# A decoder layer with product-key experts on one NeuronCore: lists of expert rows in three classes instead of two, two dense rows less, and a new placing of gathers

## The chip, the cores and the metric

The kernel runs on one core of a Trainium2 chip. The metric is the device time of one execution in microseconds. Five engines work side by side, each in its own order: TensorE (PE in the profile, its weight loads PEld), VectorE (DVE), ScalarE (ACT), GpSimd (POOL) and SyncE (SP). SP, ACT and POOL also issue DMAs; gathers of rows by index are issued by POOL.

## The reference

One post-norm decoder layer on 256 tokens of 2048 features, all float32: attention of two kinds, an output projection with layer norm, then a product-key expert layer (PEER) with its layer norm, then a gated embedding with a third. The change touches the expert layer alone:

```python
va, ia = lax.top_k(sa, PEER_TOPK)          # 16 of 128 row keys, per token and head
vb, ib = lax.top_k(sb, PEER_TOPK)          # 16 of 128 column keys
top, sel = lax.top_k(cand, PEER_TOPK)      # 16 of the 256 sums
eidx = jnp.take_along_axis(cidx, sel, axis=-1)     # expert = ia * 128 + ib
gates = jax.nn.softmax(top, axis=-1)
act = jax.nn.gelu(jnp.einsum('thed,td->the', u[eb], xb))
out = jnp.einsum('the,thed->td', gates * act, v[eb])
```

There are 128 x 128 = 16,384 experts, each with one row of `u` and one of `v` (2048 float32, 8 KB). A token uses 8 heads x 16 experts.

## The kernel before, in words

The kernel treats the tokens in two ways. The first 88 tokens (`NSP`) are **sparse**: for each the 128 rows of `u` and of `v` are gathered by index, 128 rows at a time, and multiplied on VectorE (`sparse_work`, lines 1015 and 1025); that is 88 gathers of `u` rows and 88 of `v` rows (line 1049). A generator hands them out, and the numbers `GQ`, `GU`, `GUF`, `GUT`, `GUL`, `GUE` and `GV` say how many gathers are put into the order after each block of PE's work (`gathers(n)` adds n to an account and issues whole ones). Four buffers `gb` hold them, and the use of a gather is put into the order when the third one behind it is issued.

The other 168 tokens (`NDT`) are computed on TensorE, for all experts at once: 40 of them (`N0`) lie in the first tile of 128 tokens, 128 in the second. For every expert, W = gelu(u . x) times the token's gate (zero where the token did not choose it), and the output is the sum of W times `v`. In stages:

- **Dense u rows.** For the first `SEG1` of the 128 values of `ia`, all 128 experts are computed: one load of 1 MB, then 16 matmuls of 168 columns (`u_block`, line 223). Each float32 matmul is two instructions in the profile. The results stay in `A0` and `A1`.
- **Lists.** Beside that stage `list_work` counts which experts the 168 tokens really use, and packs their numbers densely into lists, 128 to a block (`idxV`). Part 1 covers the values of `ia` that were not computed densely, part 0 those that were. Experts used by second-tile tokens alone go into the first class, whose blocks need 128 columns; the experts that a first-tile token uses go into the second class, whose blocks take all 168 columns. `CAPS` fixes how many blocks each class has: `((24, 15), (30, 18))`. If a list overflows, a branch near the end (`tc.If(more > 0)`) computes what is left; with these inputs it is not taken.
- **u list.** For part 1, each block's `u` rows are gathered (`uf`, line 1412), transposed on TensorE (16 transposes, line 1453), copied out by ScalarE (`uT`, line 1456), and multiplied with the tokens (line 1462). ScalarE's gelu goes into `WL` (line 1494). Between these, `all_gates` works in small steps, `run(work, 1)`: `gate_work` turns the choices of three tokens at a time into one-hot matrices on VectorE (`eq`, `ohb`, line 717; `lo`, line 1105) and ScalarE (`hi`, line 1103), multiplies them on TensorE (lines 1114, 1115), and scales `A0`, `A1` or `WL` by the gates (line 1123). Then `A0` and `A1` are stored to DRAM as `s_w`.
- **v lists.** First part 0, then part 1: each block's `v` rows are gathered (`vf` or `vx`), for part 0 also the rows of `s_w` that belong to them (`wc`), and TensorE adds 16 products into six PSUM banks (`v_mm`, line 1512). A class says which columns a block writes (`cols`). Row buffers are five slots shared with the weights of other stages (`WF`) and four more, `vx` (`NVX`), that open once `A0` and `A1` are gone.
- At the end of part 1, `natural_out` (line 1071) and `third_sums` (line 1083) bring the sparse tokens' sums in, and layer norm and gate follow.

A scheduler places the instructions by a model of their times, but what goes through `keep` stays in the order written, engine by engine. VectorE's uses of the gathers, the one-hot matrices, ScalarE's `hi` and `uT` copies and all gathers on POOL are such. The order around the u list is written out in this loop (from line 1483):

```python
for b in range(NBLK[1]):
    for c in range(4):
        turn(4 * b + c + 2)                  # transposes, two chunks ahead
        rows_mm(ps, turned.pop(0), c, c0, n)
        if b >= 4 and (c or n > P) and not stored:
            run(work, 1)
    keep(nc.scalar.activation(WL_of(b), ps[:, :n], AF.Gelu_apprx_tanh))
    if b >= NBLK[1] - LEAD:
        fetch()                              # a v row block ahead
    gathers(GUL[n > P] if b < NBLK[1] - LEAD - 2 else GUE)
```

## Time and profile before

| | us |
|---|---|
| median of 3 runs | 1656.95 (1654.5 to 1661.91) |
| the profiled execution's own time | 1646.54 |
| its span, first to last instruction | 1644.7 |
| PE busy | 1604.3 (98%) |
| VectorE busy | 1058.7 (64%) |
| ScalarE busy | 731.3 (44%) |
| POOL busy | 583.1 (35%) |
| mean granted TensorE clock | 0.988 |

By the trace, dense u rows run from 532 to 813 us, the u list from 813 to 1139, the first v list from 1143 to 1319, the second from 1319 to 1536. The profile was taken of one execution; PE's busy time counts overlapping instructions once. A row of the order of time reads: start, length, engine, line, operation, output and inputs, shape, count of merged instructions, and in brackets the engine's idle time before it with what ended it. In shapes, "128*128 128x168" is a weight tile of 128 by 128 and 168 columns that stream through it. A row with a window has its start and end, its length, and the busy time and count of each engine named, then PEclk (the clock that TensorE was granted, 1.00 is full), the DMA engines' busy share and the GB/s they moved.

### The profile page before, as it was taken

To read this page: it belongs to the slowest core of one execution; us is meant where nothing else is said; L and a number is where in the kernel's file an instruction comes from. 1 tells how busy PE (TensorE), PEld (TensorE's weight loads), DVE (VectorE), ACT (ScalarE), POOL (GpSimd) and SP (SyncE) were. 2 spreads that over 40 slices of the span, in tenths; PEclk is the share of its full clock that TensorE was granted. 3 is DMA by queue.
4 is the path that set the end of the run, shared out by engine and by line. 5 is a ranking of instruction groups with operands and counts; after the bars stand their busy time and mean duration, and the time that the engine had idled before them with its cause. 6 is when DMAs were issued, how large, how long until landed. Compare 5 with 4: busy or idle time off the path is not lost. (4 is left out here: it accounts for less than half of the span.)

```text
span 1644.7 us, 30592 instructions
## 1 busy us (share of the span) xinstructions
PE 1604.3 (98%) x11666; PEld 1488.5 (91%) x11666; DVE 1058.7 (64%) x2557; ACT 731.3 (44%) x1740; POOL 583.1 (35%) x542
## 2 busy tenths in 40 slices
PE   9999999999999999999979999998899999999998
PEld 7888888888888999999979999998799999999786
DVE  5555588865378899577668778855476533341777
ACT  5587458753201264857646666632142000000543
POOL 0133123200233423322463434455878564440000
PEclk9999999999999999999989999999999999999999
DMA  8644654475799799999999999998999999996671
GB/s 295 203 157 162 230 172 142 154 287 187 282 409 412 285 421 403 410 375 385 371 387 376 343 349 355 360 401 356 408 406 384 366 402 420 421 402 210 214 260 51
DMA packets 90614, 518.53 MB, mean 315 GB/s; under 512 B 12308, under 2 KB 15444, under 8 KB 38322
## 3 DMA queue, kind: packets, MB, share of 16 engines
q0 software_dynamic: 47984, 330.83, 51.0%
q1 hardware_dynamic: 40750, 182.55, 30.4%
q10 hardware_dynamic: 1728, 3.15, 0.5%
q8 instruction: 92, 1.51, 0.4%
q14 instruction: 60, 0.49, 0.1%
HBM read 508.47 MB, written 10.18 MB: 315 GB/s over the span
## 5 line engine op out<-in xcount | busy, mean ns | idle before, releaser
L133 DVE TENSOR_TENSOR wl<-wf,wh 128x1024 fp32r<-128x1024 f32 (+1 forms) x199 | 212.8, 1092 | 126.9 <-ACT wh L132 125.5
L132 ACT CAST wh<-wf 128x1024 fp32r<-128x1024 f32 (+1 forms) x199 | 172.1, 892 | 243.3 <-DMA wf<-ple_gate 129.5
L1025 DVE SCALAR_TENSOR_TENSOR y<-gb,ew,y 128x2048 f32<-128x2048 f32 x78 | 183.2, 2349 | 127.7 <-DMA gb<-v_rows,eig 127.0
L223 PE MATMUL ps_u<-XF,wf 128*128 128x168 f32 x1632 | 251.1, 310 | 0.0
L223 PEld LDWEIGHTS ps_u<-XF,wf 128*128 128x128 f32 x1632 | 234.6, 190 | 2.2 <-DMA s_gl<-gl 0.2
L1462 PE MATMUL ps_u<-XF,uT 128*128 128x128 f32 (+1 forms) x1536 | 223.9, 290 | 0.2 <-ACT uT L1456 0.2
L1015 DVE SCALAR_TENSOR_TENSOR gb<-gb,xq 128x2048 f32<-128x2048 f32 x88 | 200.7, 2285 | 28.0 <-DMA gb<-u_rows,eig 27.9
L1462 PEld LDWEIGHTS ps_u<-XF,uT 128*128 128x128 f32 x1536 | 202.1, 193 | 0.7 <-ACT uT L1456 0.3
L1512 PE MATMUL ps_v<-WL,vf 128*128 128x128 f32 (+1 forms) x1536 | 196.1, 290 | 3.9 <-DMA vf<-v_rows,idxV 3.6
L1512 PEld LDWEIGHTS ps_v<-WL,vf 128*128 128x128 f32 x1536 | 193.7, 194 | 5.5 <-DMA vf<-v_rows,idxV 4.5
L1049 POOL DMA_INDIRECT gb<-u_rows,eig x88 | 99.6, 1132 | 242.6 <-DVE gb L1015 59.7
L211 PE MATMUL ps_qk<-X,wh 128*128 128x512 f32 x512 | 185.2, 401 | 0.0
L1456 ACT COPY uT<-ps_T 128x512 f32<-128x512 f32 x192 | 111.7, 586 | 106.3 <-PE ps_T L1453 106.1
L1103 ACT ACTIVATE hi<-eq,ghf 128x56 f16<-128x56 f16 (+2 forms) x336 | 87.3, 326 | 138.6 <-DVE eq L717 117.8
L213 PE MATMUL ps_qk<-X,wl 128*128 128x256 f32 x512 | 145.7, 285 | 0.0
L1412 POOL DMA_INDIRECT vf<-v_rows,idxV x73 | 93.9, 1286 | 120.6 <-PE ps_v L1512 88.2
L1049 POOL DMA_INDIRECT gb<-v_rows,eig x88 | 117.5, 1336 | 53.8 <-issue 20.7
L1453 PE MATMUL ps_T<-ident,uf 128*128 128x128 f32 x768 | 116.2, 276 | 5.8 <-ACT WL L1494 5.8
L211 PEld LDWEIGHTS ps_qk<-X,wh 128*128 128x128 f32 x512 | 96.4, 188 | 22.0 <-issue 1.0
L1512 PE MATMUL ps_v<-wc,vf 128*128 128x128 f32 (+1 forms) x800 | 107.3, 293 | 8.2 <-DMA vf<-v_rows,idxV 8.2
L223 PE MATMUL ps_q<-XF,wf 128*128 128x256 f32 x512 | 113.5, 379 | 0.0
L1512 PEld LDWEIGHTS ps_v<-wc,vf 128*128 128x128 f32 x800 | 102.6, 194 | 8.4 <-DMA vf<-v_rows,idxV 8.4
(366 smaller groups left out, 2859.3 us busy)
## 6 DMA issues: line engine op xcount, KB each, us to landing
wf<-peer_u SPq DMA_DIRECT2D x51, 1024.0 KB
wf<-w_qk SPq DMA_DIRECT2D x64, 512.0 KB
wf<-w_out SPq DMA_DIRECT2D x32, 512.0 KB
wf<-peer_wq SPq DMA_DIRECT2D x16, 1024.0 KB
wf<-ple_gate SPq DMA_DIRECT2D x16, 1024.0 KB
wf<-w_v SPq DMA_DIRECT2D x16, 512.0 KB
wf<-w_sv SPq DMA_DIRECT2D x15, 512.0 KB
early<-peer_u SPq DMA_DIRECT2D x5, 1024.0 KB
```

The costliest lines, as they stand in the source:

```text
L132: self.order(nc.scalar.copy(wh, src))
L133: self.order(nc.vector.tensor_tensor(wl, src, wh.bitcast(F32), op=ALU.subtract))
L211: nc.tensor.matmul(ps, wh[:, j * P:(j + 1) * P], xt[:, dt, :], start=dt == 0, stop=False)
L213: nc.tensor.matmul(ps[:, :T], wl[:, j * P:(j + 1) * P], xt[:, dt, :T], start=False, stop=dt == ND - 1)
L223: nc.tensor.matmul(ps[:, :T - t0], wf[:, dt * P:(dt + 1) * P], xt[:, dt, t0:], start=dt == 0, stop=dt == ND - 1)
L1015: keep(nc.vector.scalar_tensor_tensor(g, g, 1.0, xq[i], op0=ALU.mult, op1=ALU.mult, accum_out=eact[i][:, j:j + 1]))
L1025: keep(nc.vector.scalar_tensor_tensor(ys[i], g, ew[i][:, j:j + 1], ys[i], op0=ALU.mult, op1=ALU.add))
L1049: keep(nc.gpsimd.indirect_dma_start(out=g, out_offset=None, in_=a[kind], in_offset=bass.IndirectOffsetOnAxis(ap=eig[i][:, 0, j:j + 1], axi ...
L1453: nc.tensor.transpose(ps[:, j * P:(j + 1) * P], uf[:, (4 * c + j) * P:(4 * c + j + 1) * P], ident)
L1456: keep(nc.scalar.copy(uT, ps))
L1462: nc.tensor.matmul(ps[:, :n], uT[:, j * P:(j + 1) * P], XF[:, d, NSP + c0:NSP + c0 + n], start=d == 0, stop=d == ND - 1)
L1512: return nc.tensor.matmul(o, vf[:, d * P:(d + 1) * P], w, start=False, stop=last and (d % 3 == 2 or d == ND - 1))
```

## The change

- **Three classes.** A list now has experts used by second-tile tokens alone (blocks of 128 columns), by first-tile tokens alone (40 columns), and by both (168 columns), in this order (`SPAN`). Masks `m16`, `cols`, `used` and `inn` get a third layer; `CAPS` becomes `((23, 5, 10), (31, 7, 12))`, in blocks 38 and 50 for 39 and 48. `scale` gets the column at which a class begins, since classes 1 and 2 are adjacent for first-tile tokens, and classes 0 and 2 are not.
- **54 dense u rows** (`SEG1`) for 56.
- **Gathers.** Sparse gathers are left out in the first three u list blocks, and their paces change: `GUL` (1.28, 1.58) for (1.10, 1.50), `GUE` 1.75 for 2.20, `GV` (0.45, 0.82), (0.42, 0.98) for (0.42, 0.80), (0.42, 0.85). A 40-column block has the pace of a 128-column one.
- **High gate parts.** The three ScalarE multiplies that make `hi` are issued by `high` after the step's first `yield`, behind the next four transposes and eight matmuls, instead of together with `eq`.
- **First weight gathers.** `A0` and `A1` are closed and the first `wc` gathers issued after the last but one u list block, instead of after the last.
- **v slots.** The four `vx` buffers take the fifth to eighth v blocks instead of the sixth to ninth; four pairs of v and weight gathers instead of five go out ahead of the v loop.

The fallback branch is adapted to the new counts.

```diff
-SEG1 = 56
+SEG1 = 54
-CAPS = ((24, 15), (30, 18))
+CAPS = ((23, 5, 10), (31, 7, 12))
+NCL = len(CAPS[0])
+SPAN = ((N0, P), (0, N0), (0, NDT))
-GUL, GUE = (1.10, 1.50), 2.20
-GV = (0.42, 0.80), (0.42, 0.85)
+GUL, GUE = (1.28, 1.58), 1.75
+GV = (0.45, 0.82), (0.42, 0.98)
...
-        keep(nc.vector.scalar_tensor_tensor(m16[:, 0], n01[:, P:], 1.0, m16[:, 1],
-                                            op0=ALU.min, op1=ALU.subtract))
-        keep(nc.vector.tensor_scalar(m16[:, 0], m16[:, 0], 0.0, None, op0=ALU.max))
+        for k, op in ((2, ALU.mult), (0, ALU.subtract)):
+            keep(nc.vector.scalar_tensor_tensor(m16[:, k], n01[:, P:], 1.0, m16[:, 1 if k else 2],
+                                                op0=ALU.min, op1=op))
+        keep(nc.vector.tensor_tensor(m16[:, 1], m16[:, 1], m16[:, 2], op=ALU.subtract))
...
-            for j in range(n):
-                t = slice(t0 + j, t0 + j + 1)
-                keep(nc.scalar.mul(hi[:, j, :], eq[:, j, :], ghf[:, t]))
...
-            return ohb, hi, lo
+            return ohb, hi, lo, eq
+        def high(t0, n, hi, eq):
+            for j in range(n):
+                keep(nc.scalar.mul(hi[:, j, :], eq[:, j, :], ghf[:, t0 + j:t0 + j + 1]))
...
             yield
+            if group is not None:
+                _, hi, _, eq = made[-1][1]
+                high(*group[:2], hi, eq)
...
-        yield from gate_work(oh, aT, bT, [(NSP, P, nA, nB, ((WB, NSP),)),
-                                          (P, T, 0, nA + nB, ((WA, P), (WB, NSP)))])
+        s0 = at[1] - at[1] % 2
+        yield from gate_work(oh, aT, bT, [
+            (NSP, P, s0, nb + nb % 2 - s0, [(W[k], NSP, at[k] - s0) for k in (1, 2)]),
+            (P, T, 0, nb + nb % 2, [(W[0], P, 0), (W[2], NSP, at[2])])])
...
-        for k in range(2):
+        for k in range(NCL):
             keep(nc.tensor.matmul(ps[:ns, k * P:(k + 1) * P], m[:, k], ones16,
                                   start=True, stop=True))
...
     def cols(i, b):
-        return (N0, P) if b < CAPS[i][0] else (0, NDT)
+        k = 0
+        while b >= CAPS[i][k]:
+            b -= CAPS[i][k]
+            k += 1
+        return SPAN[k]
...
-        if k >= WF and not i and b < NBLK[0] - WF:
+        if LEAD <= k < LEAD + NVX and not i and b < NBLK[0] - WF:
             vf = vxp.tile([P, D], F32, name="vx", tag="vx", bufs=NVX)
...
-        gathers(GUL[n > P] if b < NBLK[1] - LEAD - 2 else GUE)
+        if b >= 3:
+            gathers(GUL[n > P] if b < NBLK[1] - LEAD - 2 else GUE)
+        if b == NBLK[1] - 2:
+            assert stored
+            pools.close("a1p", "a0p")
+            vxp = pools.open("vxp", "right", bufs=1)
+            wcp = pools.open("wcp", "right", bufs=1)
+            with tc.issue_after(behind.ins):
+                weights()
     pools.close("utp")
-    assert stored
-    pools.close("a1p", "a0p")
-    vxp = pools.open("vxp", "right", bufs=1)
-    wcp = pools.open("wcp", "right", bufs=1)
     with tc.issue_after(behind.ins):
         weights()
-        for _ in range(NVX + 1):
+        for _ in range(NVX):
             fetch()
             weights()
```

More of the change, by code (lines that the diff above doesn't have):

```diff
@@ L1233, in list_work @@
         ps = pbank(pa, "ps_cols")
-        for k in range(2):
+        for k in range(NCL):
             keep(nc.tensor.matmul(ps[:ns, k * P:(k + 1) * P], m[:, k], ones16,
                                   start=True, stop=True))
-        cols = oh.tile([P, 2 * P], F16, name="cols", tag="cols")
-        keep(nc.vector.tensor_copy(cols[:ns], ps[:ns, :2 * P]))
+        cols = oh.tile([P, NCL * P], F16, name="cols", tag="cols")
+        keep(nc.vector.tensor_copy(cols[:ns], ps[:ns, :NCL * P]))
         yield
         ps = pbank(pa, "ps_used")
-        for k in range(2):
+        for k in range(NCL):
             o, c = ps[:, k * (ns + 1):(k + 1) * (ns + 1)], cols[:ns, k * P:(k + 1) * P]
@@ L1246, in list_work @@
         yield
-        used = oh.tile([P, 2, SEGX + 1], F32, name="used", tag="used")
+        used = oh.tile([P, NCL, SEGX + 1], F32, name="used", tag="used")
         keep(nc.vector.tensor_copy(
             used[:, :, :ns + 1],
-            ps[:, :2 * (ns + 1)].rearrange("p (k a) -> p k a", k=2)))
+            ps[:, :NCL * (ns + 1)].rearrange("p (k a) -> p k a", k=NCL)))
         pos = oh.tile([P, SEGX], F32, name="pos", tag="pos")[:, :ns]
         rank = oh.tile([P, SEGX], F32, name="rank", tag="rank")[:, :ns]
-        inn = oh.tile([P, 2, SEGX], F32, name="inn", tag="inn")[:, :, :ns]
+        inn = oh.tile([P, NCL, SEGX], F32, name="inn", tag="inn")[:, :, :ns]
         lf = left[:, s0:s0 + ns]
-        ov = gin.tile([P, 2], F32, name=f"ov{part}")
+        ov = gin.tile([P, NCL], F32, name=f"ov{part}")
         keep(nc.vector.tensor_tensor(lf, m[:, 0], m[:, 1], op=ALU.add))
-        for k in range(2):
+        keep(nc.vector.tensor_tensor(lf, lf, m[:, 2], op=ALU.add))
+        for k in range(NCL):
             u = used[:, k, :ns]
@@ L1261, in list_work @@
             keep(nc.vector.tensor_tensor(lf, lf, inn[:, k], op=ALU.subtract))
-            keep(nc.vector.scalar_tensor_tensor(u, u, float(k * caps[0] * P) - BIG, inn[:, k],
+            keep(nc.vector.scalar_tensor_tensor(u, u, float(sum(caps[:k]) * P) - BIG, inn[:, k],
                                                 op0=ALU.add, op1=ALU.mult))
@@ L1268, in list_work @@
                                             op0=ALU.add, op1=ALU.add))
-        if len(over) > 2:
+        keep(nc.vector.tensor_tensor(pos, pos, used[:, 2, :ns], op=ALU.add))
+        if len(over) == 2 * NCL:
             for o in over[1:]:
@@ L1397, in build @@
     wlp = pools.open("wlp", "left", bufs=1)
-    WL = wlp.tile([P, CAPS[1][0] * P + CAPS[1][1] * NDT], F32, name="WL")
+    WL = wlp.tile([P, sum(n * w for n, (_, w) in zip(CAPS[1], SPAN))], F32, name="WL")
     lkp = pools.open("lkp", "left", bufs=1)
@@ L1418, in WL_of @@
     def WL_of(b):
-        c0 = min(b, CAPS[1][0]) * P + max(b - CAPS[1][0], 0) * NDT
+        c0 = sum(cols(1, k)[1] for k in range(b))
         return WL[:, c0:c0 + cols(1, b)[1]]
```

40 lines of the change are left out of this document (22 added, 18 removed).

## The prediction

> **What bounds the kernel now.** I read the page's sums and slices first, then the windows of the three list stages, then the order of time around each hole in PE.
>
> ```profile
> span 1644.7 us, 30592 instructions
> PE 1604.3 (98%) x11666; PEld 1488.5 (91%) x11666; DVE 1058.7 (64%) x2557; ACT 731.3 (44%) x1740; POOL 583.1 (35%) x542
> PEclk9999999999999999999989999999999999999999
> DMA  8644654475799799999999999998999999996671
> ...
> 812.70:1143.29 330.59, 315.92 (x3184) 310.44 (x3183) 241.10 (x738) 183.34 (x489) 151.73 (x116) 0.97 0.95 370
> 1143.29:1319.45 176.16, 167.99 (x1580) 166.90 (x1575) 95.19 (x284) 40.14 (x159) 128.17 (x100) 0.98 0.97 383
> 1319.45:1471.00 151.55, 147.78 (x1227) 146.42 (x1226) 60.00 (x39) 4.43 (x8) 77.20 (x61) 0.99 1.01 413
> ```
>
> The windows hold, in this order, length, busy time of PE, PEld, DVE, ACT and POOL, the granted clock, the DMA share and GB/s. PE sets the end: it works for 98% of the span, so the change is priced on PE. But the list stages (u list from 812.7, first v list from 1143.3, second from 1319.5) also move 370 to 413 GB/s with the 16 DMA engines 95 to 101% busy, so bytes are the next limit. PE has four real holes there:
>
> ```profile
> 841.93:850.66 8.73, 0.00 (x1) 0.69 1.01 427
> 850.66:855.53 4.87, 4.69 (x33) 0.50 1.02 422
> 1108.92:1113.56 4.64, 0.01 (x2) 0.78 1.03 432
> 1113.56:1118.36 4.80, 4.80 (x19) 0.50 1.01 427
> 1157.83:1166.01 8.18, 0.01 (x1) 0.80 1.00 372
> 1166.01:1169.56 3.55, 3.55 (x16) 0.50 1.03 429
> 1356.63:1360.00 3.37, 0.00 (x2) 1.00 1.01 413
> 1360.00:1364.12 4.12, 4.12 (x22) 0.59 1.02 426
> ```
>
> Here only PE's busy time is listed. Each hole costs twice: after it PE runs some 3 to 5 us at clock 0.50, and half of that is lost. I call them A = 8.7 + 2.4 = 11.1 us, B = 4.6 + 2.4 = 7.0, C = 8.2 + 1.8 = 10.0, D = 3.4 + 1.7 = 5.1; together 33 us.
>
> **Prices on PE.** A float32 matmul is two instructions; with 16 tiles of the 2048 features a block is 32 instructions.
>
> ```profile
> 829.57 1.47 PE L1453 MATMUL ps_T<-ident,uf 128*128 128x128 f32 x12
> 1309.76 9.85 PE L1512 MATMUL ps_v<-wc,vf 128*128 128x168 f32 x68
> 1319.45 18.03 PE L1512 MATMUL ps_v<-WL,vf 128*128 128x128 f32 x160
> ...
> 1511.07 0.39 PE L1083 MATMUL ps_y<-sel,gb 128*128 128x32 f32 x2
> ...
> 1513.97 0.39 PE L1083 MATMUL ps_y<-sel,y 128*128 128x32 f32 x2
> ...
> 1514.95 0.61 PE L1083 MATMUL ps_y<-sel,gb 128*128 128x32 f32 x2
> ...
> 1517.94 0.61 PE L1083 MATMUL ps_y<-sel,y 128*128 128x32 f32 x2
> ```
>
> The instructions overlap, so I take distances between starts, leaving about 0.3 us for the last one's tail. 168 columns: (9.85 - 0.31) / 67 = 0.142 us, a block 4.56 us. 128 columns: (18.03 - 0.29) / 159 = 0.112, a block 3.57. A block's 16 transposes: 16 x (1.47 - 0.28) / 11 = 1.75. The new class has 40 columns, which no list block has now; the nearest row is the sum of the sparse tokens, with 32. Thirteen pairs take 1513.97 - 1511.07 = 2.90 us, 0.112 us an instruction: **a 32-column matmul takes exactly as long as a 128-column one**. With 40 between two equal ends, a 40-column block is 3.57 us at full clock. So the narrow class saves 1.0 us against a 168-column block, not three quarters of it, and nothing against a 128-column one.
>
> **The sum on PE.** Capacities are in blocks: before (24, 15) and (30, 18), after (23, 5, 10) and (31, 7, 12).
> - Dense u rows 56 to 54: -2 x 4.56 = -9.1 us.
> - u list: blocks at 3.57 us go from 30 to 31 + 7 = 38, those at 4.56 from 18 to 12, and two more blocks are transposed: 28.6 - 27.4 + 3.5 = +4.7.
> - First v list: 24 to 28 at 3.57, 15 to 10 at 4.56: 14.3 - 22.8 = -8.5.
> - Second v list: 30 to 38 and 18 to 12: 28.6 - 27.4 = +1.2.
> - The lists' own eight more float16 matmuls, of at most 128 columns: between 0 and 0.9 (0.112 each); I take +0.5.
>
> Together -11.2 us. The bytes hardly change: counted from the reference's inputs, u rows gathered grow by 208 of 8 KB (+1.7 MB), two dense loads of 1 MB go, and v rows stay 10,954.
>
> ```profile
> L1259 DVE SCALAR_TENSOR_TENSOR inn<-used,m 128x72 f32<-128x72 f32 (+1 forms) x4 | 0.9, 215 | 0.0
> L1047 POOL COPY pace<-mark 1x1 f32<-1x1 f32 x71 | 28.3, 398 | 0.5
> ```
>
> VectorE gets about 15 more operations of 0.2 us for the third class, in the dense stage where it works 44 of 62.7 us; PE's 4.6 us per dense block hides them. If that cover were gone, the lists would be 3 us late and so would the first row gather. The dense stage also ends 9 us sooner, under the tail of the second list:
>
> ```profile
> 750.00:812.70 62.70, 61.98 (x485) 59.47 (x485) 43.97 (x136) 44.99 (x147) 21.91 (x27) 1.00 0.97 377
> 791.08 1.05 POOL L1412 DMA_INDIRECT uf<-u_rows,idxV  x1 [0.61 <-PE ps_u L223]
> 818.93 1.17 PE L1453 MATMUL ps_T<-ident,uf 128*128 128x128 f32 x9
> 819.94 0.27 PE L1297 MATMUL ps_list<-blk,row 128*128 128x80 f16 x3
> ```
>
> The first row gather waits for a buffer that a dense block frees, so it comes earlier with it; list products already run between transposes. I charge 0, at most the 9 us.
>
> **The holes.** What stands in front of each:
>
> ```profile
> 847.70 2.29 DVE L1015 SCALAR_TENSOR_TENSOR gb<-gb,xq 128x2048 f32<-128x2048 f32 x1 [2.67 <-DMA gb<-u_rows,eig]
> 850.27 0.80 ACT L1103 ACTIVATE hi<-eq,ghf 128x56 f16<-128x56 f16 x3 [11.65 <-DVE eq L717]
> 850.98 0.56 ACT L1456 COPY uT<-ps_T 128x512 f32<-128x512 f32 x1
> ...
> 1110.12 2.35 DVE L1025 SCALAR_TENSOR_TENSOR y<-gb,ew,y 128x2048 f32<-128x2048 f32 x1 [4.88 <-DMA gb<-v_rows,eig]
> 1112.60 0.71 ACT L1103 ACTIVATE hi<-eq,ghf 128x18 f16<-128x18 f16 x3 [7.30 <-DVE eq L717]
> ...
> 1132.73 3.02 POOL L1412 DMA_INDIRECT wc<-s_w,idxW  x1 [0.30 <-issue]
> 1157.78 1.00 POOL L1412 DMA_INDIRECT vf<-v_rows,idxV  x1 [0.30 <-issue]
> ```
>
> **A and B** are one mechanism. VectorE's order is fixed: the use of a late sparse gather stands ahead of the one-hot `eq`; on ScalarE `hi` waits for `eq`, and behind `hi` waits the copy that empties PE's transposes. The change puts `hi` one step later in the order. A step is 4 transposes and 8 matmuls, 0.4 + 0.9 = 1.3 us, so this alone saves at most 1.3 us a hole; it can cost nothing, as the product that needs `hi` comes two groups later. More comes from the gathers: none in the first three u blocks (A), and in the last six 1.75 a block for 2.20 (B). One gather is 128 rows of 8 KB, 1.05 MB: a 168-column block of 6.3 us with 2.2 gathers and a row block wants 3.36 MB, 530 GB/s; with 1.75 it is 2.9 MB, 455, nearer to the 432 that the hole's row shows as the most. I take A from 11 to 4 and B from 7 to 2, -12; ends 0 and -18.
>
> **C**: the fifth v block's gather is issued at 1157.78, 25 us behind the first weight gather, and its bytes let PE go at 1166.0. After, the first three weight gathers are issued one u block (6.3 us) earlier, the fifth to eighth v blocks have buffers of their own (before: the sixth to ninth), and one pair of v and weight gathers less stands in POOL's queue. The gather then comes perhaps 10 us after the last u block, while zeroing and four blocks cover 19 us. I take 10 to 2, -8; ends 0 and -10. Late next is the ninth block, whose gather goes into a freed buffer and has four blocks (14 us) more of cover. What the earlier weight gathers can cost: they read the stored gates, and if those were late, every later gather of POOL would stand behind them.
>
> **D** is saturation, and that grows. The second v list at 413 GB/s has its gathers issued by block 36 of 48; by the new paces it is block 43 of 50: of 176 gathers 69 go ahead of the u list (71 paced ones before, in the row above, less two blocks' 0.92), 35 x 1.28 + 6 x 1.58 + 6 x 1.75 = 65 in it, 28 x 0.45 + 10 x 0.82 = 21 in the first v list, and the 21 left go at 0.42 and 0.98 a block (18 left before). 43 row blocks and 21 gathers are 67 MB, about 3 more in flight, in 38 x 3.57 + 5 x 4.56 = 158 us and some 4 of other PE work: 430 GB/s. I charge D 5 to 9, +4 (ends -5 and +12). The first v list needs 64 MB in 160 us, 403 GB/s, which still fits.
>
> Holes together -16. **Forecast:** -11 - 16 = -27 us. The profiled execution took 1646.54 us (span plus 1.8), the median of the runs 1656.95, 10.4 above it; I take the difference over: 1630.
>
> **The rivals. 1: the clock falls in the narrow v blocks.**
>
> ```profile
> 1357.30:1360.71 3.41, 0.71 (x6) 1.00 1.02 418
> 1510.90:1514.31 3.41, 3.41 (x33) 1.00 0.62 259
> 1514.31:1517.72 3.41, 3.41 (x18) 0.50 0.00 0
> 1155.90:1159.32 3.42, 1.93 (x18) 1.00 1.00 358
> 1521.14:1524.55 3.41, 3.41 (x13) 0.50 0.00 0
> ```
>
> PE was busy without a gap in 1510.90 to 1514.31, yet the clock then went to 0.50: some 31 instructions of 32 columns, 990 columns in 3.41 us, count as idle, like the six of 128 columns (770) of the first row, before the drop at 1360.71. Fifteen or more of 128 (1920 columns and up, the fourth row) kept it at full. A 40-column run makes 30.6 x 40 = 1220: between the two, nearer to what fell. If it falls, an instruction takes 0.213 us (seven pairs from 1514.95 to 1517.94), so a block 6.83. Five blocks (17.9 us) in the first list and seven (25) in the second, the first 3.4 us of each free, the rest 1.91 times as long, and 3 us of wide work at half clock behind: 13.2 + 1.5 + 19.7 + 1.5 = 36 us. 1630 + 36 = 1666, slower than before. It decides as soon as the limit lies above 1220 columns. For it: the position. Against it: the gate matmuls and the four sums of natural tokens between these blocks lift some of them. [...]
>
> **2: it falls in the narrow u blocks too.** There 16 transposes stand beside the 32 matmuls. If they count, the share is over half and nothing falls; if not, it is 32 x 40 columns in 5.3 us, 820 per 3.41 us, below what fell. Price: seven blocks of 5.3 us, 33.8 us beyond the first 3.4, almost doubled: +32, so 1698 with rival 1. [...] No row of before has transposes with so little beside them that it would tell.
>
> **3: bytes are the bound already.** The holes then only move: each gather saved early is one more later. The list stages keep their lengths but for PE's -11: 1646. For it: 413 GB/s and a full DMA row; against it: the u stage at 370.
>
> **4: the lists overflow** and a loop over all 128 rows runs (128 x 4.6 us and more). The reference's inputs fill the six classes to 89 to 99% (2874, 572, 1218 and 3914, 869, 1507 of 128 x capacity), with nothing over.
>
> **Chances.** Forecast 0.58, rival 1 0.20, rival 2 0.05, rival 3 0.16, rival 4 0.01. About 0.5% (8 us) is what a measurement tells from no change. Faster: nearly all of the forecast and 0.7 of rival 3, 0.68. Same: the rest of rival 3, some of the forecast, half of rival 1, 0.16. Slower: 0.16. The forecast's own range is 1612 to 1645; the whole one is taken to 1607 (all holes gone) and 1668 (rival 1).
>
> **What would show it.** Starts of 40-column matmuls 0.112 us apart (0.213 if the gate falls); PEclk 1.00 in both narrow runs; no hole over 3 us at the start of the u list or before the fifth v block; the second v list at 415 to 430 GB/s with short waits for `vf`. I am wrong if PE's clock drops there or the holes reappear at the same sum.

## The result, and the profile after

The changed kernel takes 1676.99 us (median of 6 runs, 1671.68 to 1679.03) against 1658.16 us for the kernel before on the same chip (6 runs, 1654.5 to 1663.68): ratio 1.0106, 95% interval 1.0086 to 1.0125. It is slower by 1.1%; 1630 was forecast, and 1677 lies above the range's upper end of 1668.

Chips differ here. The kernel of before took 1658 to 1660 us on the first chip of the experiments, 1651 on a second, 1647 on a third and 1648 on a fourth; the pair above has the times of the first. On the fourth chip the changed kernel took 1656.53 us against 1647.95, ratio 1.0049 (1.0030 to 1.0069). The sign holds on both, the size does not. So comparisons below name the chip.

The page of the changed kernel, its sums and its slices, where every digit of the last two rows is one fortieth of the span:

```profile
span 1677.2 us, 30775 instructions
PE 1638.6 (98%) x11738; PEld 1520.2 (91%) x11738; DVE 1060.5 (63%) x2586; ACT 738.9 (44%) x1748; POOL 588.6 (35%) x542
...
PEclk9999999999999999999899999999987999768999
...
DMA  7544644485899899999799999999986899967571
```

PE is again busy for 98%, but now with 1638.6 us, 34 more than before, for work that was to be 11 us less. This profiled execution took 1679.03 us. Busy time that grows with no more work to do points at the clock, whose mean fell from 0.988 to 0.962. In the PEclk row it dips at the seam of the dense rows and the u list (8), and longer in the first (8, 7) and the second v list (7, 6, 8).

The two fourth-chip profiles, one of each kernel, are the cleanest pair for the budget. The windows are the stages of the prediction, bounded by PE's first transpose, the first matmul of each v list, and the last one: dense u rows (from 557 us), u list, first v list, second v list, rest. The columns are those of the prediction's windows. First before:

```profile
557.00:818.40 261.40, 257.52 (x1940) 251.84 (x1939) 197.06 (x537) 163.60 (x515) 85.79 (x107) 0.99 0.97 382
818.40:1150.00 331.60, 316.77 (x3184) 311.21 (x3181) 241.09 (x738) 183.47 (x489) 151.62 (x117) 0.97 0.95 369
1150.00:1326.00 176.00, 168.31 (x1573) 167.23 (x1574) 95.11 (x284) 40.10 (x159) 125.86 (x100) 0.98 0.97 383
1326.00:1539.40 213.40, 208.69 (x1651) 207.19 (x1651) 77.83 (x67) 11.88 (x23) 90.22 (x67) 0.98 0.90 358
```

And the changed kernel there, with the two stretches of 40-column blocks cut out below its stages:

```profile
557.00:809.80 252.80, 248.16 (x1866) 242.70 (x1865) 189.78 (x525) 153.24 (x479) 81.73 (x101) 0.99 0.95 378
809.80:1135.40 325.60, 318.59 (x3300) 313.32 (x3298) 246.10 (x763) 202.91 (x533) 168.88 (x124) 0.98 0.96 384
1135.40:1312.30 176.90, 175.00 (x1547) 173.78 (x1544) 96.15 (x299) 40.78 (x159) 119.69 (x95) 0.89 0.93 361
1312.30:1550.80 238.50, 234.14 (x1716) 231.89 (x1715) 82.24 (x69) 11.84 (x23) 89.97 (x71) 0.87 0.85 340
```
```profile
1232.00:1266.00 34.00, 34.00 (x203) 33.87 (x203) 17.83 (x66) 10.25 (x39) 19.53 (x18) 0.50 0.90 351
1433.00:1481.00 48.00, 48.00 (x219) 46.81 (x218) 16.08 (x17) 0.00 (x0) 9.75 (x10) 0.51 0.66 247
```

The dense stage is 8.6 us shorter and the u list 6.0, as forecast in sum. The first v list, which was to become 16 us shorter, is 0.9 longer; the second is 25.1 longer. Together that is +11.4, the difference of the two spans (1648.3 and 1659.6) to a tenth. In both v lists PE is almost never idle (175.0 of 176.9 us, 234.1 of 238.5), and the mean clock is 0.89 and 0.87. The last two rows say where: 34 and 48 us without one idle microsecond, at half the clock.

### The profile page after: what moved, and what is told of

The parts are those of the page before. It is cut to its first block, busy times and chain, and to the rows that moved or that the text cites. A ratio compares the mean times of both kernels' runs of the same rounds, so it can differ in the third digit from the quotient of the medians.

```text
span 1677.2 us, 30775 instructions
## 1 busy us (share of the span) xinstructions
PE 1638.6 (98%) x11738; PEld 1520.2 (91%) x11738; DVE 1060.5 (63%) x2586; ACT 738.9 (44%) x1748; POOL 588.6 (35%) x542
## 4 chain that ended last, share of the span: by engine, by line
PE 83%; DMA 5%; DVE 3%; another core or an unknown queue 2%; issue 2%; ACT 2%; POOL 2%; POOLq 0%; ACTq 0%; SPq 0%; DVEq 0%
PE ps_v L1533 15%; PE ps_u L225 14%; PE ps_u L1479 11%; PE ps_qk L213 7%; PE ps_q L225 7%; PE ps_T L1470 5%; PE ps_qk L215 4%; PE ps_v L232 2%; PE ps_v L234 2%; PE ps_v L233 2%; DMA vf<-v_rows,idxV 2%; PE ps_gate L232 1%; PE ps_gate L234 1%; PE ps_gate L233 1%
## 5 line engine op out<-in xcount | busy, mean ns | idle before, releaser
L225 PE MATMUL ps_u<-XF,wf 128*128 128x168 f32 x1568 | 240.7, 310 | 0.0
L225 PEld LDWEIGHTS ps_u<-XF,wf 128*128 128x128 f32 x1568 | 225.2, 190 | 2.1
L1479 PE MATMUL ps_u<-XF,uT 128*128 128x128 f32 (+2 forms) x1600 | 223.9, 284 | 0.0
L1533 PEld LDWEIGHTS ps_v<-WL,vf 128*128 128x128 f32 x1600 | 217.4, 213 | 5.1 <-DMA vf<-v_rows,idxV 3.4
L1533 PE MATMUL ps_v<-WL,vf 128*128 128x128 f32 (+2 forms) x1600 | 218.3, 304 | 3.3 <-DMA vf<-v_rows,idxV 3.2
L1429 POOL DMA_INDIRECT vf<-v_rows,idxV x74 | 103.6, 1399 | 141.2 <-PE ps_v L1533 119.6
L1113 ACT ACTIVATE hi<-eq,ghf 128x54 f16<-128x54 f16 (+2 forms) x336 | 87.9, 328 | 139.1 <-DVE eq L719 136.4
L1052 POOL DMA_INDIRECT gb<-v_rows,eig x88 | 109.5, 1244 | 54.9 <-issue 20.1
L1533 PE MATMUL ps_v<-wc,vf 128*128 128x128 f32 (+2 forms) x768 | 118.0, 314 | 7.1 <-issue 6.7
L1533 PEld LDWEIGHTS ps_v<-wc,vf 128*128 128x128 f32 x768 | 110.3, 214 | 9.2 <-issue 9.1
```

Of the source, the lines that this page charges most:

```text
L225: nc.tensor.matmul(ps[:, :T - t0], wf[:, dt * P:(dt + 1) * P], xt[:, dt, t0:], start=dt == 0, stop=dt == ND - 1)
L1052: keep(nc.gpsimd.indirect_dma_start(out=g, out_offset=None, in_=a[kind], in_offset=bass.IndirectOffsetOnAxis(ap=eig[i][:, 0, j:j + 1], axi ...
L1479: nc.tensor.matmul(ps[:, :n], uT[:, j * P:(j + 1) * P], XF[:, d, NSP + c0:NSP + c0 + n], start=d == 0, stop=d == ND - 1)
L1533: return nc.tensor.matmul(o, vf[:, d * P:(d + 1) * P], w, start=False, stop=last and (d % 3 == 2 or d == ND - 1))
```

## The experiments

The theory to test was rival 1: 40-column matmuls, issued without a gap, stream so little that the clock is lowered. The first rival theory was that the placing of gathers and slots is at fault and the clock only follows.

**Wider and narrower blocks (wide128, wide48, wide64).** The u list keeps its 40-column blocks; in the v lists they are multiplied WIDE columns wide, the further ones being zeros. The second weight tile gets the room and is cleared:

```diff
+WIDE = 128                        # 48 and 64 in the other two
+KEPT = (P, WIDE, NDT)
...
-    WL = wlp.tile([P, sum(n * w for n, (_, w) in zip(CAPS[1], SPAN))], F32, name="WL")
+    WL = wlp.tile([P, sum(n * w for n, w in zip(CAPS[1], KEPT))], F32, name="WL")
+    W1 = WL[:, CAPS[1][0] * P:CAPS[1][0] * P + CAPS[1][1] * WIDE]
+    keep(nc.gpsimd.memset(W1.rearrange("p (b t) -> p b t", t=WIDE)[:, :, N0:], 0.0))
...
-        return SPAN[k]
+        return (0, WIDE) if k == 1 and used else SPAN[k]
```

> The changed kernel with one thing altered: in both v lists the 12 blocks of 40 columns are multiplied 128 columns wide, the 88 further columns being zeros (in the first list the gathered weights are zero there anyway, in the second the weight tile is cleared there once). The blocks of the u list stay 40 wide. Theory 1 (the 40-column blocks stream too little and the granted clock falls): a 128-column matmul took 0.112 us and the 40-column one no less, so nothing is added, the granted clock stays at 1.0 through 1231-1300 and 1446-1494 us, the profile's clock goes back from 0.962 to about 0.985, and some 35 us go (13 to 17 in the first v list, 20 to 24 in the second): 1642 us, 1634 to 1650. Theory 2 (the lists are late because of where gathers and slots were put, or wait for bytes, and the clock falls because TensorE waits): the same 1677 us, within 5, with the clock still low in those stretches.

> The same edit with 48 columns instead of 128. The windows of the changed kernel's trace put the point at which the clock falls between a share of streaming of 0.36 (40 columns, which fell) and 0.40 to 0.42 (windows that stayed or came back); 48 columns would be a share of about 0.43. Theory 1 with the limit just above 40 columns: as with 128 columns, 1642 us, 1634 to 1650. Theory 1 with a limit well above: the clock falls as before and the time stays near 1677. Theory 2 (the placing, not the width): 1677, within 5.

> The 40-column v blocks multiplied 64 columns wide, to place the point at which the clock falls: 48 columns fell and 128 held. One look at the clock in 1240-1290 and 1446-1495 us: if it stays, the limit lies between 48 and 64 columns and the time is that of 128 columns, 1644 to 1656; if it falls, the limit lies between 64 and 128 and the time is 1672 to 1684.

Measured on the first chip: 128 columns 1651.61 us, ratio to before 0.9958 (0.9937 to 0.9979); 48 columns 1679.7, ratio 1.0148 (1.0123 to 1.0173). One run of 64 columns on the second chip took 1623.89 us, where before took 1651.07. With 128 columns there is more arithmetic, and the kernel takes 25 us less, 1.6 us above the range expected; the clock holds in both stretches:

```profile
1245.00:1280.00 35.00, 34.26 (x337) 33.93 (x336) 19.79 (x70) 10.27 (x39) 23.00 (x18) 1.00 0.88 313
1430.00:1480.00 50.00, 50.00 (x424) 49.45 (x424) 20.80 (x22) 0.00 (x0) 26.59 (x19) 1.00 1.00 402
```

So theory 1 holds for 128 columns, and theory 2 falls. The point at which the clock falls lies higher than I had read from the windows: I had expected 48 columns to be above it, and they fell just as 40 did. Single windows of 3.4 us, with each one's matmuls and then the granted clock, show where it lies. (In the first profiles of both kernels the changes of the clock are whole multiples of 3.41 us apart: ten before, the first at 845.30 and the last 199 multiples later at 1524.55 us, and sixteen in the changed kernel, from 817.90 to 1558.59, 217 multiples. With 48 columns 1244.4, 1278.5 and 1452.7 us fit this too. The windows lie between two such points. A window's counts take in matmuls that reach over its edges.) 40 columns (changed kernel, first profile, 1442.6 to 1446.0 us; the next windows are at half clock; the two 128-column matmuls reach in from the block before):

```profile
L1533 PE MATMUL ps_v<-WL,vf 128*128 128x40 f32 x31 | 3.6, 282 | 0.0
L1533 PE MATMUL ps_v<-WL,vf 128*128 128x128 f32 x2 | 0.4, 275 | 0.0
```

48 columns, the matmuls of 1449.30 to 1452.70, then the clock of that window and of the next:

```profile
L1537 PE MATMUL ps_v<-WL,vf 128*128 128x48 f32 x32 | 3.8, 277 | 0.0
...
1449.30:1452.70 3.40, 3.40 (x32) 3.40 (x32) 0.00 (x0) 0.00 (x0) 0.99 (x1) 0.99 1.01 422
1452.70:1456.10 3.40, 3.40 (x17) 3.10 (x16) 0.73 (x2) 0.00 (x0) 1.11 (x2) 0.50 1.01 417
```

64 columns, the matmuls of 1226.50 to 1229.90 and the two clocks:

```profile
L1537 PE MATMUL ps_v<-wc,vx 128*128 128x64 f32 x33 | 3.8, 275 | 0.0
...
1226.50:1229.90 3.40, 3.40 (x33) 3.40 (x32) 2.02 (x12) 2.37 (x9) 2.75 (x3) 1.00 1.01 417
1229.90:1233.30 3.40, 3.40 (x42) 3.40 (x41) 1.04 (x6) 0.43 (x2) 2.53 (x3) 1.00 0.99 387
```

All three widths issue 31 to 33 matmuls a window, so a narrower matmul is no faster. Some 1500 columns a window (32 x 48) let the clock go here, some 2100 (33 x 64) kept it, and so did the 1920 of the prediction's row. Once the clock is low, a matmul takes twice as long here, and so a window holds half the columns: the 40-column rows of a low and a high stretch, changed kernel (v list 1255 to 1275 us, u list 1000 to 1040), have 14.7 us for 64 instructions, 0.23 each, and 23.2 for 188, 0.12 each.

```profile
L1533 PE MATMUL ps_v<-wc,vf 128*128 128x40 f32 x64 | 14.7, 414 | 0.0
```
```profile
L1479 PE MATMUL ps_u<-XF,uT 128*128 128x40 f32 x188 | 23.2, 272 | 0.0
```

**64 columns once more (wide64_again)**, on the first chip.

> The kernel with 64-column v blocks, timed in rounds. Theory (the 40-column clock was worth 25 us or more): 25 to 40 us below the changed kernel on the same chip, and below the kernel of before by 0.4 to 1.7%. Rival (the one look was a lucky one): within 1% of the changed kernel.

Measured 1651.61 us (1642.93 to 1662.1, in two groups of five, near 1645 and near 1659), ratio 0.9949 (0.9917 to 0.9982), 29 us below the changed kernel beside it (1680.96). But its profile, of an execution of 1656.13 us, has the low clock in the first v list:

```profile
1235.00:1247.40 12.40, 11.03 (x121) 10.89 (x120) 6.30 (x22) 3.16 (x12) 8.46 (x8) 1.00 1.00 376
1247.40:1278.10 30.70, 30.70 (x176) 30.70 (x176) 14.52 (x51) 7.89 (x30) 14.97 (x11) 0.50 0.65 222
```
```profile
L1120 PE MATMUL ps_G<-hi,ohb 128*128 128x50 f16 x9 | 0.9, 184 | 1.4 <-DVE WL L1127 1.4
```

A wait of 1.4 us for VectorE (the second fence, 1243 to 1250 us) thinned out one window; from then on the clock stayed at 0.50 until 1278.1 us, where the 168-column blocks come. At 0.213 us a matmul, the prediction's figure from a stretch at half clock, 16 fit into a window, with 64 columns 1024 in all; from 1250 to 1275 us there are 109 of them, beside 42 of 50 columns in float16, and the clock did not come back. With 128 columns 16 a window are 2048. After such a window (before, 1360.71 to 1364.12 us, at 0.50, 16 begin in it) the clock was at 1.00, and the profile of wide128 has no stretch like this one. So 64 columns kept the clock here but did not regain it. The profiles of the two other runs with 64 columns on the first chip (wide64_56 and wide64_best, below) show the same: behind waits of 1.9 and 0.9 us the clock is at 0.50 for 23.9 and 34.1 us. The two groups of times fit executions with and without this fall: the mean clock of the five slower ones is 0.975 to 0.981, of the five faster ones 0.984 to 0.988, and 30.7 us at half clock lower the mean over 1654 us by 0.009. The faster ones have no profile, so it is not shown.

**Mixing instead of widening (pairs).** Each 40-column block shares its matmuls with a 168-column one, one after the other, by a permutation of the v order:

```diff
+        mixed = [x for j in range(a1) for x in (a0 + j, a0 + a1 + j)]
+        PERM.append(list(range(a0)) + mixed + list(range(a0 + 2 * a1, a0 + a1 + a2)))
...
+            if cols(*block[:2])[1] == N0:
+                waiting.append(block)
+            else:
+                group, k = waiting + [block], 4 if waiting else 8
...
+                for d in range(ND):
+                    for x in group:
+                        v_mm(d, *x, False)
```

> The changed kernel with the order of the v blocks altered and nothing else: each 40-column block is multiplied together with a 168-column block, one matmul of the one after one of the other, so that no stretch of a window holds 40-column matmuls alone (0.112 and 0.142 us, 104 columns in the mean). All widths, bytes and matmuls are the same; the reach of the prefetch is shorter by one block while a pair waits. Theory 1 (clock by the work in a window): the clock stays, 1642 us, 1634 to 1655 (the upper end if the shorter reach costs some gathers' waits). Theory 2 (the fall comes with the 40-column shape itself, or with the placing): 1677 or more.

Measured 1657.58 us, ratio 0.9999 (0.9980 to 1.0019), just above the range expected but 19 us below the changed kernel, with not one column added. In the second list the clock stays at 1.00, so the shape itself is not at fault:

```profile
1235.00:1283.00 48.00, 42.90 (x392) 42.56 (x390) 23.82 (x88) 13.42 (x51) 24.60 (x21) 0.93 0.77 276
1440.00:1500.00 60.00, 60.00 (x478) 59.33 (x478) 26.66 (x22) 0.00 (x0) 26.61 (x24) 1.00 1.01 413
```

In the first list PE idles 5 of 48 us, most of it in one wait of 3.8 us for VectorE's scaling by gates. That list takes 191.7 us, in wide128 182.5, while the second takes 223.2 and 222.8: the 6 us above wide128 were lost in the first list. That the scaling comes late because its steps now come in lumps is argued, not shown.

**Each half of the change alone (place, place_again, classes).** "place" is the kernel before with the placing edits; "classes" is the changed kernel with them undone.

```diff
 place: GUL, GUE, GV, high(), "if b >= 3", first weights() one block early, LEAD <= k < LEAD + NVX; CAPS, SEG1 as before
 classes: three classes, SEG1 = 54, CAPS ((23, 5, 10), (31, 7, 12)); the lines above as before
```

> The kernel of before with the placing half of the change alone: high gate parts moved behind the yield, sparse gathers of the u list from its fourth block on and at the new paces, weight gathers issued two blocks before the u list's end, extra v slots at the new turn. Lists, widths and dense rows are those of before. Theory P1 (the placing does what the prediction said): holes A and B go (11 and 7 us) and C shrinks from 10 to about 2, D may grow by 4: 1658 - 16 to -20, 1638 to 1644. Theory P2 (the placing brings the new short gaps at the start of the first v list, some 7 us with their cold clock, in place of C): A and B go, C's time stays: 1645 to 1650. Rival (the gain of A and B is lost again to gathers that come too early): 1655 to 1660.

> The placing half alone, again. Theory P1 (the short gaps are of the chip and come with the early weights there): on the first chip gaps of 0.4 to 1.4 us between groups of four matmuls in the first 50 us of the first v list, and a gain of 8 to 14 us in place of the 20 on the second chip. Theory P2 (they come with the three classes): no such gaps, and the same 20 us, ratio 0.986 to 0.990.

> The changed kernel with the placing half undone: three classes, 54 dense rows, 40-column blocks, but high gate parts, sparse gathers, paces, first weight gathers and v slots as before. Theory (the clock in the 40-column blocks costs some 25 us as the wider blocks showed, the seam some 10, the shorter lists and dense rows save 11): 1658 - 11 + 25 + 10 = 1682, with the holes A, B and C back: 1678 to 1694. Rival (the placing is what made the changed kernel slow): under 1660.

Placing alone is faster: 1631.09 us on the second chip, ratio 0.9894 (0.9860 to 0.9929), and 1633.88 on the third, 0.9909 (0.9890 to 0.9928), a gain of 13 to 20 us (theory P1 had 14 to 20). place_again was to tell what the placing does on the first chip; it ran on the third, so its two theories stay undecided. Classes alone are slower on the second chip, 1685.12, ratio 1.0222 (1.0187 to 1.0258), with the clock at 0.50 for 34.1 us of the first v list and 47.8 of the second. So the low clock comes with the classes, and the rival that the placing slowed the kernel falls. What the holes were worth can be read from PE's idle column in the u list, before (fourth chip, window 818.4 to 1180), then in place_again's windows of the u list and both v lists; last come the matmuls that zero the output banks, in the u list of place_again and in that window of before:

```profile
L1453 PE MATMUL ps_T<-ident,uf 128*128 128x128 f32 x768 | 116.2, 276 | 5.6 <-ACT WL L1494 5.6
L1512 PE MATMUL ps_v<-wc,vf 128*128 128x128 f32 x160 | 20.4, 294 | 7.9 <-DMA vf<-v_rows,idxV 7.7 <-DMA wc<-s_w,idxW 0.3
...
L1114 PE MATMUL ps_G<-hi,ohb 128*128 128x56 f16 (+1 forms) x174 | 19.0, 189 | 8.8 <-DVE lo L1105 8.8
```
```profile
817.40:1126.20 308.80, 308.80 (x3171) 305.06 (x3170) 235.47 (x736) 186.64 (x489) 167.55 (x118) 1.00 0.99 392
1126.20:1299.70 173.50, 168.51 (x1585) 165.98 (x1583) 93.05 (x285) 40.10 (x159) 125.60 (x97) 1.00 0.97 383
1299.70:1525.10 225.40, 215.71 (x1650) 213.41 (x1651) 84.45 (x71) 11.82 (x23) 90.76 (x70) 0.95 0.88 349
```
```profile
L1526 PE MATMUL ps_v<-zero,ident 128*128 128x504 f32 x6 | 2.7, 586 | 0.0
L1518 PE MATMUL ps_v<-zero,ident 128*128 128x504 f32 (+1 forms) x12 | 4.7, 539 | 0.0
```

Before waits 8.8 us (hole A), 5.6 (B with one shorter wait) and 7.9 (C). With the placing A and B are gone to the last microsecond, and the u list takes 308.8 us for 331.6, that is 22.8 us less. Of these 2.0 are only moved: six of the twelve zeroing matmuls now stand behind the list's end (2.7 us of them in it for 4.7). The other 20.8 are still more than the 18.1 that I had counted for both holes. In the second v list the placing gives some back (225.4 us for 213.4): PE waits 8.3 us for v rows there, where before waits 3.4, and the clock is 0.95 for 0.98.

**The seam (seg56, wide_seam).** Between the dense rows and the u list a hole stands that I had charged at nothing (changed kernel, fourth chip: PE's groups of 819 to 831 us, then that window and the 9 us ahead of it):

```profile
L1310 PE MATMUL ps_list<-blk,row 128*128 128x76 f16 x25 | 3.0, 229 | 6.6 <-ACT row L891 3.6 <-DVE eqb L719 2.8 <-ACT blk L1321 0.2
...
809.80:819.00 9.20, 9.20 (x90) 9.12 (x88) 4.45 (x15) 8.94 (x26) 2.88 (x5) 1.00 1.00 392
819.00:831.00 12.00, 4.99 (x38) 3.53 (x37) 6.99 (x22) 10.28 (x31) 2.05 (x3) 0.65 0.64 229
```

The list products of part 0 wait for the one-hots, and ScalarE makes half of those for the rows: it is busy 19.2 of 21.2 us. "seg56" gives the two dense rows back; "wide_seam" is wide128 with twelve one-hots moved to VectorE:

```diff
-SEG1 = 54;  CAPS = ((23, 5, 10), (31, 7, 12))
+SEG1 = 56;  CAPS = ((24, 5, 10), (30, 7, 12))        # seg56
-            if ia % (2 * GB):
+            if ia % (2 * GB) and (part or ia < 30):      # wide_seam
```

> The changed kernel with 56 dense u rows as before the change, and with the list capacities that go with them (24, 5, 10 and 30, 7, 12 blocks). Two dense blocks more cost 9.1 us, one u block less gives 3.6. Theory S1 (the gaps of about 10 us between the dense blocks and the u list, 813 to 823 us, come from the two dense blocks that used to cover the last of the list work on ScalarE): the gaps go, 1677 + 9.1 - 3.6 - 10 = 1672 us, 1668 to 1676. Theory S2 (they come from the third class's own work in the lists, whatever the number of dense rows): the gaps stay and the time is 1677 + 5.5 = 1682, 1679 to 1686. The clock in the 40-column blocks of the v lists falls as in the changed kernel by either.

> The kernel with 128-column v blocks, and in the work that makes the first v list the last four groups of row one-hots moved from ScalarE to VectorE (twelve one-hots). Theory (ScalarE is the engine that is late at the seam: it was busy 27 of 30 us there while VectorE had 13 of 30 idle): the gaps of 820 to 830 us shrink from 7 us to 3 or less with less cold clock behind them, 1651.6 - 6 to -9, 1642 to 1646. Rival (the seam waits for the order of the products, whoever makes them): unchanged, 1648 to 1654.

seg56 took 1670.8 us, ratio 1.0093 (1.0069 to 1.0116), 6 to 10 us below the changed kernel on the first chip, and the same products wait for nothing there:

```profile
L1310 PE MATMUL ps_list<-blk,row 128*128 128x80 f16 x19 | 2.2, 200 | 0.0
```

So the two dense blocks had been the cover of the list work's end (theory S1). The u list of seg56 is not free of holes for that: a wait of 3.8 us for VectorE (`lo`) stands near its end, about where B was. wide_seam took 1626.2 us on the second chip, 0.9870 (0.9829 to 0.9911). Its expected time was for the first chip, and wide128 was not run on the second, so the nearest comparison is the single run of 64 columns there (1623.89), and it is no faster. Its products waited 4.7 us for VectorE in place of 6.6 for both: the lateness moved to the other engine. Against that run its u list is 2.9 us shorter (322.9 us) and its second v list 2.9 longer (225.5), with 9.5 us of waits for v rows there in place of 6.8.

**Short gaps on one chip (after_again, late, after_third, before_again, before_third).** In the first v list PE's groups, 1137 to 1180 us in the first profile of the changed kernel and 1142 to 1185 on the fourth chip:

```profile
L1533 PE MATMUL ps_v<-wc,vf 128*128 128x128 f32 x133 | 22.0, 318 | 7.1 <-issue 6.7
```
```profile
L1533 PE MATMUL ps_v<-wc,vf 128*128 128x128 f32 x232 | 27.2, 276 | 0.0
```

The same code waits 7.1 us, in gaps of 0.3 to 1.4 us, for nothing that the profile shows, or not at all. "late" is the changed kernel with the first weight gathers behind the u list as before, the others are the two kernels unchanged.

```diff
-        if b == NBLK[1] - 2:          # pools closed and opened, first weights() here
-        for _ in range(NVX):
+        for _ in range(NVX + 1):      # late: all of it behind the loop, as before
```

> The changed kernel itself once more, beside the next three on one chip, since the kernel of before took 1658 us on one chip and 1651 on another, and the run of short gaps at the start of the first v list stood in every profile of the early-weights placing from the first chip and in none from the second. Theory (the clock in the 40-column blocks is the loss on every chip): slower than before, by 15 to 25 us on a chip like the first, by 5 to 15 on a chip like the second, where the short gaps are missing. Rival (the loss is one chip's short gaps): no slower than before where the gaps are missing.

> The changed kernel with the first weight gathers, and the pools that they need, behind the u list again, as in the kernel before; all else is the change. Theory L1 (the early gathers bring the short gaps): the short gaps go and a wait of 7 to 10 us for v rows stands in the first 30 us of the first v list as before; the time is that of the changed kernel within 5 us. Theory L2 (the short gaps are of the chip or of the three classes): they stay, and a wait for v rows comes beside them: 3 to 10 us slower than the changed kernel.

> The kernel of before, one more profile. If the execution is a typical one of 1655 to 1662 us, it shows 8 to 15 us more than the first profile in one or two places: a wait for a dense u row with a cold clock behind it near 665 us (it stood in the profiles of three other kernels, whose code is the same there), or short gaps at the start of the first v list.

> The changed kernel once more. On a chip where before takes 1647 to 1651 us: no short gaps, 1656 to 1664 us, ratio 1.005 to 1.010, the loss in the 40-column v blocks still there. On the chip where before takes 1658 us: 1677 to 1681 with the short gaps. Rival (the change is no slower where the gaps are missing): ratio 1.000 or less.

> The kernel of before once more. On the chip where it takes 1658 us: the short gaps of 0.4 to 1.4 us stand at the start of its first v list too, or 3 to 10 us stand near 665 us; if neither does and the time is 1646, the profile is an execution apart. On another chip: 1645 to 1651 and no short gaps.

after_again, first chip: 1680.96 us, ratio 1.0116 (1.0076 to 1.0157), gaps present. late, third chip: 1659.79, ratio 1.0078 (1.0061 to 1.0094), no gaps, and no wait for v rows in the first 50 us either, so on that wait L1 and L2 both miss: the early weight gathers were not what removed hole C. What the theories say of the gaps stays open, since no other profile of that chip has gaps either. after_third, fourth chip: 1656.53, ratio 1.0049, no gaps. before_again, third chip: 1644.8, no gaps; before_third, fourth chip: 1650.12, no gaps, but a wait of 3.2 us at 665 for a dense row, which also stands in after_third. In all, the gaps stand in every one of the nine profiles of the early placing with three classes that have the first chip's times, and in none of the six with that placing on the other three chips. So they go with that chip. The first v list of the changed kernel takes 194.7 and 197.2 us in the two profiles with the gaps and 176.9 in the one without; against the kernel before, the changed kernel loses some 10 us more on the first chip than on the fourth. What they are, and whether the kernel before has them on that chip (its 10 us above the other chips would fit), stays open: none of its three profiles shows them, and the two whose chip is known are from other chips.

**Versions meant to beat both (wide64_56, wide_seg56, wide64_best).**

```diff
 wide64_56:   64-column blocks, SEG1 = 56, CAPS ((24, 5, 10), (30, 7, 12))
 wide_seg56:  128-column blocks, the same
 wide64_best: 64-column blocks, the seam edit, GV second pair (0.34, 1.25) for (0.42, 0.98)
```

> 64-column v blocks with 56 dense u rows and capacities 24, 5, 10 and 30, 7, 12. Two dense blocks more cost 9.1 us, one u block less gives 3.6, the seam's gaps (some 7 to 10 us) go: 1 to 5 us below wide64_again. Rival (the bytes of the v lists set the end): the same time as wide64_again, within 2 us, with more waits for gathers in the second v list.

> Three classes with v blocks of the second tile 128 columns wide, 56 dense rows and capacities 24, 5, 10 and 30, 7, 12. Theory (64 columns hold the clock but cannot bring it back once a wait has let it fall, 128 columns can; and the seam is covered): on the first chip the clock is back within 10 us of each wait in the first v list, and the time is 5 to 12 us below that of 64 columns with 56 rows: ratio to before 0.983 to 0.988. Rival (the bytes set the end of the lists): ratio 0.989 to 0.991, as with 64 columns.

> 64-column v blocks, the last four groups of row one-hots on VectorE, and in the second v list fewer sparse gathers beside the narrow blocks (0.34 in place of 0.42 a block) and more beside the wide ones (1.25 in place of 0.98). The seam gave 3 us in one profile, and the waits for gathers in the second list were some 7 us there: 3 to 10 us below wide64_again. Rival (the second list stands at 411 to 421 GB/s, so waits only change place): within 2 us of wide64_again.

wide64_56 took 1646.09 us on the first chip, ratio 0.9899 (0.9856 to 0.9943), 5.5 below wide64_again, where 1 to 5 were expected. wide_seg56 took 1621.58 on the third, where before took 1647.12: 0.9848 (0.9832 to 0.9865), the best of the study with an interval. That is within the ratio expected, but what was expected of the first chip was not tested, since it ran on another. Its stages from the u list on:

```profile
813.60:1131.00 317.40, 311.39 (x3224) 307.28 (x3222) 239.81 (x744) 190.40 (x499) 172.19 (x125) 0.99 0.97 388
1131.00:1294.40 163.40, 163.10 (x1585) 161.37 (x1584) 93.11 (x297) 40.68 (x159) 116.04 (x94) 1.00 0.99 395
1294.40:1507.40 213.00, 207.06 (x1684) 204.94 (x1683) 82.27 (x69) 11.82 (x23) 95.30 (x70) 0.98 0.91 369
```

The first v list is at 163.4 us and full clock. wide64_best is a miss: 1661.1 us, ratio 1.0000, 9.5 above wide64_again. The sparse gathers that I moved to the wide blocks came too late for the sums at the end, and PE stood 11 us for VectorE (window 1505 to 1530):

```profile
L1603 PE MATMUL ps_y<-ident,XF 128*128 128x128 f32 x2 | 0.7, 448 | 11.1 <-DVE XF L1551 11.1
```

## Why the prediction was wrong

**The clock: the step that failed is the choice of the forecast over rival 1.** Rival 1 was the right mechanism in the right place, and I gave it 0.20. The row that I had, 990 columns of 32-column matmuls whose next window was at half clock, lay nearer to the 1220 of a 40-column run than the row of 1920 that held, as the prediction itself said; against it I set only gate matmuls and four natural sums that "lift some of them". They did not: the first list's stretch has such gate matmuls too, and the clock stayed at 0.50 for its 34 us. By the windows above and that row the limit lies between some 1500 and 1920 columns of float32 a window. Its price was nearly right in the first list: 14.7 us forecast, and the changed kernel's 176.9 us (fourth chip) against 161.1 for 64 columns at full clock (second chip) are 15.8. In the second list 21.2 were forecast and 16 to 19 came: 238.5 against 222.6 and 219.1 with 64 columns. There the full clock meets waits for v rows (6.8 us with 64 columns on the second chip), so part of what the clock costs DMA would have cost anyway. On one chip, 128 columns brought back 25 to 29 of the forecast 36. Forecast and rival 1 together say before - 27 + 36 = +9 us; measured +8.6 on the fourth chip, and 19 to 21 on the first, where the short gaps come on top. That the sum fits the fourth chip so closely is in part luck, since in the u list two errors of 9 to 10 us cancel.

**Dense rows: right.** -9.1 forecast, -8.6 measured (261.4 to 252.8 us).

**The u list: right in sum, wrong in both terms.** +5 for blocks and list matmuls, -12 for A and B, gave -7; measured -6.0. But A and B gave 20.8 (place_again, without the zeroing that only moved), past my end of -18. Of these, 14.8 us are time without work on PE in the list before (331.6 less 316.8), where I had counted 13.3 for the two holes; the other 6.0 are busy time, for 4.8 of lost clock counted. Above all I expected a part of each hole to stay (4 and 2 us), where the u list of place_again has none.

**The seam: the other failed step.** "I charge 0, at most the 9 us." With +5 and -20.8 the u list should have come to -15.6; it came to -6.0, so the seam cost 9.6 us, just past my upper end. Its window agrees: 7.0 of 12 us without work on PE, and a clock of 0.65, so that what PE does there takes longer. I had named the cover (dense blocks over the tail of list work) and priced VectorE alone; ScalarE, which makes half of the row one-hots and is busy 19.2 of 21.2 us there, I had not priced. Nor had VectorE room for its share: with twelve one-hots moved to it, it was the late one (wide_seam).

**C and the first v list: right.** -8.5 for narrower blocks and -8 for C gave 159.5 us; with the clock held it took 161.1. That the placing removes C is shown: in classes, without it, PE waits 7.5 us for v rows in the first v list, and with it alone (place_again) no wait for v rows stands in that list. But that list is then only 2.5 us shorter (173.5 for 176.0), or 4.5 without the moved zeroing, since some 5 us of waits, for VectorE's part of the gates, stand there instead. What I gave as C's cause was not tested apart: with the first weights late again (late) C did not return, so it is the v slots or the paces, or something that follows from them.

**D and bytes.** I charged +4. The second list with the clock held takes 219 to 223 us against the 218.6 that follow from 213.4 + 1.2 + 4. But with the placing alone it takes 221.0 and 225.4 us (place, place_again), 8 and 12 more than before with the same blocks, so +4 was low there and my upper end of 12 is reached. The changed kernel's second list stands at 420 GB/s in its first half (1340 to 1433 us, fourth chip), as forecast:

```profile
1340.00:1433.00 93.00, 92.07 (x810) 92.07 (x811) 26.77 (x15) 3.84 (x7) 47.84 (x35) 0.98 1.01 420
```

**Rival 2: false.** In the u list the 40-column matmuls stand beside transposes, and the clock held (first profile, the matmuls of 1022.70 to 1026.10, then the clock of that window and the next):

```profile
L1479 PE MATMUL ps_u<-XF,uT 128*128 128x40 f32 x21 | 2.6, 270 | 0.0
L1470 PE MATMUL ps_T<-ident,uf 128*128 128x128 f32 x12 | 1.9, 279 | 0.0
L1169 PE MATMUL ps_turn<-ident,ohb 128*128 128x128 f16 x3 | 0.3, 218 | 0.0
...
1022.70:1026.10 3.40, 3.40 (x36) 3.40 (x33) 3.36 (x7) 1.96 (x6) 2.72 (x1) 1.00 1.01 422
1026.10:1029.50 3.40, 3.40 (x45) 3.40 (x45) 3.40 (x20) 1.20 (x5) 2.15 (x3) 1.00 1.02 402
```

Without the transposes this window has 840 columns, or 1224 with the three float16 matmuls, both below the 1500 that fell; with the transposes it has 2376 and more. The clock was 1.00 in that window and in the next, so here the transposes counted for it.

**Rival 3 and the difference carried over.** Bytes did not bound the gain: place alone is 13 to 20 us faster. The 10.4 us between the profiled execution and the median, which I carried over, are of the size of the difference between chips (1647 and 1658); the first profile of before is like the third chip's (spans 1644.7 and 1643.0), but its chip is not recorded. The profiled pair alone would have shown a loss of 32.5 us, of which the medians confirm 18.8.

## What to carry to other kernels

In these runs narrow matmuls on TensorE were too little work even when they were issued without a gap: in 3.4 us 32 of 48 columns lost the clock, and 33 of 64 kept it. So count the columns that stream in each 3.4 us, and where a run of blocks falls short, widen them with zeros, which cost no time here (0.11 to 0.12 us a matmul at 40 columns as at 128), or interleave them with wide ones, which cost some 6 us more (pairs against wide128). Leave room to regain the clock, not only to keep it, because at half clock the same blocks streamed half as much (0.23 us a matmul for 0.12). When blocks are taken out of a stage, look for the work that ends last under it, and at every engine that does it.

## What the runs showed of the hardware

- A float32 matmul with a 128 by 128 weight tile took the same 0.11 to 0.12 us at 40, 48, 64 and 128 columns, and 0.23 at 40 columns with half the clock: at these widths the columns were free in time but not in clock (0.50 in the v lists at 40 and 48, 1.00 at 128).
- In windows of 3.4 us at full clock, some 1500 columns of float32 matmuls (32 of 48) were too few to keep it; 1920 and some 2100 were enough. The clock stayed low for 34 and 48 us on end while PE had no idle time.
- Four chips ran the same kernel of before at medians from 1647 to 1660 us, 0.8% apart, and one of them showed gaps of 0.3 to 1.4 us between matmuls of the changed kernel, 6 to 7 us in sum, which the profile puts down to no wait.
